# Attention operands stored per query tile, rows in alternating order, and a stepped priority for the second SwiGLU supertile's preparation

## The chip, the cores and the metric

The kernel runs on one core of a Trainium2 chip. The metric is the device time of one execution in microseconds (us). The engines are PE (TensorE: matmuls), PEld (its weight loads), DVE (VectorE), ACT (ScalarE), POOL (GpSimd) and SP (SyncE, which here issues every DMA). Each engine works through its own instruction list in order.

## The reference

One layer of a hybrid decoder trunk on x of 1 x 2048 x 1024, in float32:

```python
h = rmsnorm(x, norm1_g);  p = h @ w_in            # 1024 -> 2560 columns
u, (dq, dk, dv), (sq, sk, sv) = split(p)
a_out = pool_mixer(u)                             # 256 channels, windows 2, 4, 8, 16
# differential attention: 4 heads of two 64-wide softmax maps, 128-wide values, causal
b_out = rmsnorm((softmax(q1 k1^T) - lam * softmax(q2 k2^T)) v) * (1 - lam_init)
# stick-breaking attention: 4 heads of 64, strictly causal
c_out = rmsnorm((sigmoid(z) * prod of later (1 - sigmoid(z))) v)
x = x + concat(a_out, b_out, c_out) @ w_out
x = x + (silu(h2 @ w_gate) * (h2 @ w_up)) @ w_down   # h2 = rmsnorm(x, norm2_g), width 2816
return rmsnorm(x, final_norm_g)
```

## The kernel before

Every float32 product is made from split operands: a tile is written as a high part (rounded to fp32r) and a low part (the rest), ACT makes the first (L415), DVE the second (L416), and three matmuls (L474, L475, L476) make one product. The work is cut into query tiles of 512 rows, t = 0 to 3.

Stage one, `a1_tile`, makes the input projection for a tile: it transposes the normed x (L462) and goes through ten weight units in the order `UNITS[t]`. A unit holds 256 columns. Units 1, 2, 7 give q, units 3, 4, 8 give k, units 5, 6, 9 give v. Each half unit c ends in one PSUM bank, is split into a tile `st` of two halves (high, low), and is stored to DRAM (`q_d`, `k_d`: L611; `vd_d`, `vs_d`: L595).

Stage two, `attention`, goes through 24 pairs, six in each tile t, in the order `ORDER[t]`; this text counts them from 0, so that pairs 6 to 11 are those of t = 1. A pair is two maps of 64 channels (r = 0, 1): pairs p = 0 to 3 are differential heads, 4 and 5 are two stick-breaking heads each. `load_q` fetches q (L626), `load_kv` fetches k (L635) and v (L640, L645) for every key tile j up to t. `scores` makes a block of 128 queries (g = 0 to 3) against up to 512 keys with two matmuls: the first (L657) has the high part of q, the second (L658) the low part, and k holds its high part in partitions 0 to 63 and its low part in 64 to 127, while q's 64 rows stand twice. L700 ends a pair.

Stage three, `out_proj`, makes the output projection (L923 to L925). Stage four, `mlp`, is the SwiGLU in two supertiles of 1024 rows. A product of two by two blocks is made from seven smaller ones, so that operands are sums and differences of blocks (L961, mostly on POOL). While the gate and up products of the first supertile run, `head_out` prepares the operands of the second in 16 steps: 8 of `rows` (norm, transpose, store to `h_d`) and 8 of `operands` (load from `h_d` at L1064, subtract on POOL at L1070, split, store at L1080). `head_in` loads them later (L1098).

No order is written by hand. `Plan.op` records every operation with an estimated duration, a priority and its tiles; `Plan.schedule` plays the engines through with those estimates, takes on each engine the ready operation with the lowest priority number, and the instructions are issued in the order of the planned starts. Tiles come from rings of slots: a tile can be written when an earlier holder of its slot is no longer used. SP is in order too, so a DMA that waits holds up the DMAs behind it.

For q there are two rings of two slots, one for the high part and one for the low part. One slot of each (12 and 13) lies on the weight buffers of stage one and comes free only when stage one is done, in the course of pair 18:

```python
q0=ring([2, TQ], F32R, ("w", [31, 12])), q1=ring([2, TQ], F32R, ("w", [32, 13])),
wr=ring([4, 256], F32, ("w", R(12, 14)))      # of stage one
def dma_ns(nbytes): return max(nbytes / 360.0, 450.0)
```

Of the kernel before, what the change touches and what calls it, by code (L numbers as in the profile page):

```python
# [10 lines left out]
F32 = mybir.dt.float32  # L11
# [264 lines left out]
def hybrid_block_kernel(  # L276
# [23 lines left out]

    q_d = [dram.tile([2, P, S], F32, name=f"q_d{p}") for p in range(PAIRS)]
    k_d = [dram.tile([2, P, S], F32, name=f"k_d{p}") for p in range(PAIRS)]
    vd_d = [dram.tile([P, S // P, 2, P], F32, name=f"vd_d{p}") for p in range(DIFF_PAIRS)]
    vs_d = [dram.tile([P, S // P, 2, 64], F32, name=f"vs_d{p}") for p in range(2 * SB_PAIRS)]
    o_d = [dram.tile([KB, P, TQ], F32, name=f"o_d{t}") for t in range(NT)]
# [228 lines left out]
    def a1_tile(pl, rg, t, prio, prio_pe, first):  # L534
# [10 lines left out]
        if t == 0:  # L545
            constants(pl, {"w": rb["q1"], "h": rb["p0"]}, prio + 0.5, xs[3:])
        late = []
        for un in UNITS[t]:
# [30 lines left out]
            for c, ps in enumerate(pend):  # L579
                if un == 0:  # L580
                    late = pend
                    break
                st = rg["st"].new()
                if is_v:
                    nh, e = (2, 128) if un != 9 else (4, 64)
                    stv = lambda st=st, nh=nh: st.t.rearrange("p a (h b l e) -> p (a h) b l e", h=nh // 2, b=2, l=2)
                    pv = lambda ps=ps, nh=nh: ps.t.rearrange("p (b h e) -> p b h e", b=2, h=nh)
                    for h in range(nh):
                        split(pl, lambda h=h, stv=stv: stv()[:, h, :, 0, :], lambda h=h, stv=stv: stv()[:, h, :, 1, :],
                              lambda h=h, pv=pv: pv()[:, :, h, :], TQ // nh, True, [ps], (st, (h, 0)), (st, (h, 1)),  # L590
                              prio)
                        dst = vs_d[h] if un == 9 else vd_d[2 * (un - 5) + h]
                        pr = DIFF_PAIRS + h // 2 if un == 9 else 2 * (un - 5) + h
                        blk0 = 4 * t + 2 * c
                        pl.op("dma", dma_ns(P * 4096 // nh), lambda dst=dst, blk0=blk0, h=h, stv=stv: nc.sync.dma_start(  # L595
                            dst[:, blk0:blk0 + 2, :, :], f32(stv()[:, h])), r=[(st, (h, 0)), (st, (h, 1))],
                            w=[(m_v[pr][t], (c, h))], prio=prio)
                else:
                    isq = un in (1, 2, 7)
                    if isq:  # L600
                        pl.op("act", act_ns(TQ), lambda st=st, ps=ps: nc.scalar.mul(st.t[:, 0, :], ps.t, 0.125),
                              r=[ps], w=[(st, 0)], prio=prio)
                        pl.op("dve", dve_ns(TQ), lambda st=st, ps=ps: nc.vector.scalar_tensor_tensor(
                            st.t[:, 1, :], ps.t, 0.125, f32(st.t[:, 0, :]), ALU.mult, ALU.subtract),
                            r=[ps, (st, 0)], w=[(st, 1)], prio=prio)
                    else:
                        split(pl, lambda st=st: st.t[:, 0, :], lambda st=st: st.t[:, 1, :], lambda ps=ps: ps.t,
                              TQ, True, [ps], (st, 0), (st, 1), prio)
                    pair = {1: 0, 2: 2, 7: 4, 3: 0, 4: 2, 8: 4}[un] + c
                    dst, mk = (q_d, m_q) if isq else (k_d, m_k)  # L610
                    pl.op("dma", dma_ns(P * 4096), lambda st=st, dst=dst[pair]: nc.sync.dma_start(  # L611
                        dst[:, :, t0:t0 + TQ].rearrange("l p t -> p l t"), f32(st.t)),
                        r=[st], w=[mk[pair][t]], prio=prio)
        for c, ps in enumerate(late):
# [7 lines left out]
    def load_q(pl, rg, t, p, prio):  # L622
        q = [rg["q0"].new(), rg["q1"].new()]
        for hl in range(2):
            for dup in range(2):
                pl.op("dma", dma_ns(64 * 4096) * 1.3, lambda hl=hl, dup=dup: nc.sync.dma_start(  # L626
                    f32(q[hl].t[64 * dup:64 * dup + 64]),
                    q_d[p][hl, :, t * TQ:(t + 1) * TQ].rearrange("(r d) t -> d r t", r=2)),
                    r=[m_q[p][t]], w=[(q[hl], dup)], prio=prio)
        return q  # L630

    def load_kv(pl, rg, p, j, prio):
        k, v = rg["k"].new(), rg["v"].new()
        for hl in range(2):
            pl.op("dma", dma_ns(64 * 4096) * 1.3, lambda hl=hl: nc.sync.dma_start(  # L635
                f32(k.t[64 * hl:64 * hl + 64]),
                k_d[p][hl, :, j * TQ:(j + 1) * TQ].rearrange("(r d) t -> d r t", r=2)),
                r=[m_k[p][j]], w=[(k, hl)], prio=prio)
        if p < DIFF_PAIRS:
            pl.op("dma", dma_ns(P * 4096), lambda: nc.sync.dma_start(  # L640
                f32(v.t), vd_d[p][:, 4 * j:4 * j + 4].rearrange("p b l e -> p (b l e)")),
                r=[m_v[p][j]], w=[v], prio=prio)
        else:
            for r in range(2):
                pl.op("dma", dma_ns(P * 2048), lambda r=r: nc.sync.dma_start(  # L645
                    f32(v.t[:, r * TQ:(r + 1) * TQ]),
                    vs_d[2 * (p - DIFF_PAIRS) + r][:, 4 * j:4 * j + 4].rearrange("p b l e -> p (b l e)")),
                    r=[m_v[p][j]], w=[(v, r)], prio=prio)
        return k, v

    def scores(pl, rg, q, kt, r, g, j, t, strict, prio):
        n = TQ if j < t else (g + 1) * P
        s = rg["s"].new()
        qs = slice(g * P, (g + 1) * P)

        def qk():
            nc.tensor.matmul(s.t[:, :n], q[0].t[:, r, qs], kt.t[:, r, :n], start=True, stop=False)  # L657
            nc.tensor.matmul(s.t[:, :n], q[1].t[:, r, qs], kt.t[:, r, :n], start=False, stop=j < t)  # L658
# [3 lines left out]
        pl.op("pe", 2 * mm_ns(n) + (60 if j == t else 0), qk, r=[*q, kt], w=[s], prio=prio)  # L662
        return s, n
# [299 lines left out]
    def mlp(pl, rg, prio0):  # L963
# [72 lines left out]
        def head_out(prio):  # L1036

            def rows(b):
                xb = rg["x"].new()
# [19 lines left out]

            def operands(kk, c):  # L1060
                raw, tt = rg["x"].new([4, 256], F32), rg["x"].new([4, 256], F32)
# [21 lines left out]

            return [lambda b=b: rows(b) for b in range(8)] + [
                lambda kk=kk, c=c: operands(kk, c) for kk in range(4) for c in range(2)]

# [289 lines left out]
    def banks(ids):  # L1376
# [96 lines left out]
```

## Time and profile before

| | |
|---|---|
| runs | 2711.99, 2718.97 and 2724.35 us; median 2718.97 |
| the profiled execution's own time | 2719.03 us |
| its span in the trace | 2717.2 us, 39503 instructions |
| PE busy | 2601.9 us, 96% of the span |
| mean granted clock of PE | 0.977 of full speed |
| DVE, ACT, POOL busy | 66%, 49%, 32% |
| DMA | 454.27 MB, mean 167 GB/s |

The profile describes one execution. [...]

### The profile page before, as it was taken

The page shows a single profiled execution, that of the slowest core. Times are in us where ns is not written, and L with a number is a line of the kernel's source. Part 1 is how long each engine was busy: PE and PEld are TensorE (multiplying, and loading weights), DVE is VectorE, ACT ScalarE, POOL GpSimd, SP SyncE. Part 2 cuts the span into 40 slices and gives each one's busy share as a digit, 9 for nine tenths or more (in the row PEclk, how much of TensorE's full clock was granted, in tenths as well). Part 3 has the DMA queues.
Part 4 walks back from the last instruction along what each step waited for, and adds up shares of the span by engine and source line. Part 5 has one row for each costly group of instructions (what it writes and reads, how often), then busy time and mean ns, then how long its engine had stood idle before and what let it go on. Part 6 is the DMA issues. An engine that isn't in the chain of part 4 may idle for free.

```text
span 2717.2 us, 39503 instructions
## 1 busy us (share of the span) xinstructions
PE 2601.9 (96%) x13836; PEld 2176.7 (80%) x13836; DVE 1786.2 (66%) x3131; ACT 1319.3 (49%) x2645; POOL 870.0 (32%) x890
## 2 busy tenths in 40 slices
PE   9989989989999999999989999999999998999998
PEld 7878778877888788888978877888888886888886
DVE  6366787758887888788656666545444447558557
ACT  4365566646666666665534444323333333445444
POOL 1001212212254124133015456535454544132041
PEclk9989999989999999999999999999999999999999
DMA  6786585556564775664534457465222338335223
GB/s 217 245 251 184 160 245 160 155 155 202 153 177 147 225 203 147 192 178 161 166 118 155 155 184 239 158 220 199 101 102 97 109 129 291 118 95 194 93 90 120
DMA packets 223480, 454.27 MB, mean 167 GB/s; under 512 B 23720, under 2 KB 70952, under 8 KB 223280
## 3 DMA queue, kind: packets, MB, share of 16 engines
q1 hardware_dynamic: 223280, 451.75, 52.9%
q8 instruction: 108, 1.77, 0.3%
q14 instruction: 92, 0.75, 0.1%
HBM read 321.11 MB, written 130.55 MB: 166 GB/s over the span
## 4 chain that ended last, share of the span: by engine, by line
PE 72%; DMA 9%; DVE 9%; issue 3%; ACT 2%; POOL 1%; SPq 1%; DVEq 0%; ACTq 0%; POOLq 0%
PE bank L474 16%; PE bank L476 16%; PE bank L475 16%; DVE d L416 4%; DMA d<-q_d 4%; PE bank L657 3%; PE bank L681 3%; PE bank L658 3%; DMA d<-wo_d 2%; PE bank L924 2%; PE bank L923 2%; PE bank L925 2%; ACT d L415 1%; PE bank L562 1%; PE bank L781 1%
## 5 line engine op out<-in xcount | busy, mean ns | idle before, releaser
L474 PE MATMUL bank<-d 128*128 128x512 f32 x2296 | 919.0, 400 | 14.0 <-DVE d L1122 9.8
L476 PE MATMUL bank<-d 128*128 128x512 f32 x2296 | 910.3, 396 | 5.7 <-DVE d L416 5.4
L416 DVE TENSOR_TENSOR d<-d 128x512 fp32r<-128x512 f32 (+2 forms) x672 | 614.6, 938 | 457.5 <-ACT d L415 281.2
L475 PE MATMUL bank<-d 128*128 128x512 f32 x2296 | 909.3, 396 | 3.4 <-DVE d L416 3.4
L415 ACT CAST d<-d 128x512 fp32r<-128x512 f32 (+2 forms) x672 | 489.0, 758 | 651.0 <-PE bank L476 352.3
L961 POOL TENSOR_TENSOR d<-d 128x512 f32<-128x512 f32 x336 | 520.0, 1556 | 846.3 <-DVE d L416 622.9
L474 PEld LDWEIGHTS bank<-d 128*128 128x128 f32 x2296 | 435.7, 190 | 116.0 <-DVE d L1122 12.4
L476 PEld LDWEIGHTS bank<-d 128*128 128x128 f32 x2296 | 434.3, 189 | 110.3 <-DVE d L416 8.7
L475 PEld LDWEIGHTS bank<-d 128*128 128x128 f32 x2296 | 434.8, 189 | 101.3 <-DVE d L416 5.1
L416 DVE TENSOR_TENSOR d<-bank,d 128x512 fp32r<-128x512 f32 (+3 forms) x381 | 219.3, 603 | 139.7 <-ACT d L415 138.7
L819 POOL TENSOR_TENSOR d<-d 128x512 f32<-128x512 f32 (+3 forms) x160 | 160.4, 1003 | 397.9 <-DVE d L815 375.6
L415 ACT CAST d<-bank 128x512 fp32r<-128x512 f32 (+3 forms) x381 | 187.5, 529 | 194.0 <-PE bank L681 122.0
L729 ACT ACTIVATE d<-bank,d 128x512 f32<-128x512 f32 (+3 forms) x320 | 198.9, 627 | 128.4 <-DVE d L726 120.3
L751 POOL TENSOR_SCALAR d<-d 128x512 f32<-128x512 f32 (+3 forms) x144 | 95.8, 681 | 448.7 <-ACT d L741 318.1
L726 DVE TENSOR_REDUCE d<-bank 128x1 f32<-128x512 f32 (+3 forms) x320 | 186.9, 602 | 61.6 <-PE bank L658 31.1
L657 PE MATMUL bank<-d 128*128 128x512 f32 (+3 forms) x480 | 203.7, 425 | 24.8 <-ACT d L729 9.0
L658 PE MATMUL bank<-d 128*128 128x512 f32 (+3 forms) x480 | 181.9, 382 | 25.5 <-DMA d<-q_d 25.5
L1122 DVE TENSOR_TENSOR d<-bank,d 128x512 f32<-128x512 f32 x176 | 121.0, 687 | 116.0 <-PE bank L476 98.7
L815 DVE TENSOR_TENSOR_SCAN d<-d,bank 128x512 f32<-128x512 f32 (+3 forms) x160 | 174.3, 1090 | 19.6 <-ACT d L807 8.1
L1118 ACT COPY d<-bank 128x512 f32<-128x512 f32 x132 | 77.3, 586 | 221.7 <-PE bank L476 196.9
L681 PE MATMUL bank<-ident,d 128*128 128x128 f32 x1088 | 157.5, 279 | 3.4 <-DVE d L772 2.6
L923 PE MATMUL bank<-d 128*128 128x256 f32 x512 | 149.5, 292 | 2.8 <-DMA d<-wo_d 1.1
(133 smaller groups left out, 3593.5 us busy)
## 6 DMA issues: line engine op xcount, KB each, us to landing
d<-in_w_gu_dram SPq DMA_DIRECT2D x88, 512.0 KB, 3.5
d<-in_w_in_dram SPq DMA_DIRECT2D x80, 512.0 KB, 4.6
d<-k_d SPq DMA_DIRECT2D x120, 256.0 KB, 6.6
d<-wo_d SPq DMA_DIRECT2D x52, 512.0 KB, 6.0
d<-q_d SPq DMA_DIRECT2D x96, 256.0 KB, 6.3
d<-vd_d SPq DMA_DIRECT2D x40, 512.0 KB, 4.9
g_d<-d SPq DMA_DIRECT2D x66, 256.0 KB, 2.1
d<-g_d SPq DMA_DIRECT2D x66, 256.0 KB, 2.7
```

Source lines behind the costliest of these rows:

```text
L415: pl.op("act", act_ns(n, psum), lambda: nc.scalar.copy(hi(), src()), r=r, w=[whi], prio=prio)
L416: pl.op("dve", dve_ns(n), lambda: nc.vector.tensor_sub(lo(), src(), f32(hi())), r=[*r, *after, whi], w=[wlo], prio=prio)
L474: nc.tensor.matmul(o, a_hi, b_hi, start=first, stop=False, **kw)
L475: nc.tensor.matmul(o, a_hi, b_lo, start=False, stop=False, **kw)
L476: nc.tensor.matmul(o, a_lo, b_hi, start=False, stop=last, **kw)
L657: nc.tensor.matmul(s.t[:, :n], q[0].t[:, r, qs], kt.t[:, r, :n], start=True, stop=False)
L658: nc.tensor.matmul(s.t[:, :n], q[1].t[:, r, qs], kt.t[:, r, :n], start=False, stop=j < t)
L681: nc.tensor.transpose(tp.t[:, c:c + P], rows[qb][kb // 4].t[:, (kb % 4) * P:(kb % 4 + 1) * P], ident)
L726: pl.op("dve", dve_ns(n), lambda s=s, n=n, mc=mc, sm=sm: nc.vector.tensor_reduce(sm.t[:, mc:mc + 1], s.t[:, :n], AX, ALU.max, negate=True) ...
L729: pl.op("act", act_ns(n, True, 2), lambda s=s, n=n, e=e, mc=mc, lc=lc, sm=sm: nc.scalar.activation(e.t[:, :n], s.t[:, :n], AF.Exp, bias=sm ...
L923: nc.tensor.matmul(o, m[:, 0, cs], wh.t[:, k % 4, :], start=k == 0, stop=False)
L961: pl.op(eng, ns, lambda: en.tensor_tensor(out(), a(), b(), op), r=r, w=w, prio=prio)
```

## The change

The DRAM copies of q, k and v are made one tensor per pair and tile t, laid out as the load wants them: each partition's row is one run of 4096 bytes.

- q is no longer split into a tile of high and a tile of low parts but into two tiles by query half: h = 0 has the query blocks g = 0, 1, h = 1 has g = 2, 3, each with both parts. One ring of four slots takes the place of the two rings of two. A tile is loaded by one DMA of 128 partitions, in which each of the 64 rows is read twice, so that partitions 2d and 2d + 1 hold the same row.
- k stands in the order 2d (high), 2d + 1 (low), and is loaded by one DMA of 128 partitions where two of 64 partitions were needed. Values of the stick-breaking pairs take one load where they took two.
- The stores of q and k become two DMAs of 64 partitions (one for each r) where there was one of 128.
- In all: q loads 96 to 48, k loads 120 to 60, `vs_d` loads 40 to 20, stores of q and k 48 to 96. The bytes are the same. The estimates handed to the planner change with them, so the planner's order changes everywhere.
- `head_out`: step i of the 16 gets the priority of the first step plus i; before, all had the same.

```diff
-    q_d = [dram.tile([2, P, S], F32, name=f"q_d{p}") for p in range(PAIRS)]
-    k_d = [dram.tile([2, P, S], F32, name=f"k_d{p}") for p in range(PAIRS)]
+    q_d = [[dram.tile([2, 64, 2, 2, 256], F32, name=f"q_d{p}_{t}") for t in range(NT)] for p in range(PAIRS)]
+    k_d = [[dram.tile([64, 2, 2, TQ], F32, name=f"k_d{p}_{t}") for t in range(NT)] for p in range(PAIRS)]
...
-                    pl.op("dma", dma_ns(P * 4096), lambda st=st, dst=dst[pair]: nc.sync.dma_start(
-                        dst[:, :, t0:t0 + TQ].rearrange("l p t -> p l t"), f32(st.t)),
-                        r=[st], w=[mk[pair][t]], prio=prio)
+                    for r in range(2):
+                        pl.op("dma", dma_ns(P * 2048), lambda st=st, dst=dst[pair][t], r=r, isq=isq: nc.sync.dma_start(
+                            dst[:, :, r].rearrange("h d l t -> d h (l t)") if isq else dst[:, :, r],
+                            f32(st.t[64 * r:64 * r + 64])), r=[st], w=[(mk[pair][t], r)], prio=prio)
...
-        q = [rg["q0"].new(), rg["q1"].new()]
-        for hl in range(2):
-            for dup in range(2):
-                pl.op("dma", dma_ns(64 * 4096) * 1.3, lambda hl=hl, dup=dup: nc.sync.dma_start(
+        q = []
+        for h in range(2):
+            qh = rg["q"].new()
+            q.append(qh)
+            pl.op("dma", dma_ns(P * 4096), lambda h=h, qh=qh: nc.sync.dma_start(
+                f32(qh.t), q_d[p][t][h].rearrange("(d o) r l t -> d o (r l t)", o=1).to_broadcast([64, 2, D])),
+                r=[m_q[p][t]], w=[qh], prio=prio)
...
-        for hl in range(2):
-            pl.op("dma", dma_ns(64 * 4096) * 1.3, lambda hl=hl: nc.sync.dma_start(
+        pl.op("dma", dma_ns(P * 4096), lambda: nc.sync.dma_start(
+            f32(k.t), k_d[p][j].rearrange("d l r t -> (d l) r t")), r=[m_k[p][j]], w=[k], prio=prio)
...
-            return [lambda b=b: rows(b) for b in range(8)] + [
-                lambda kk=kk, c=c: operands(kk, c) for kk in range(4) for c in range(2)]
+            return [lambda b=b: rows(b, prio + b) for b in range(8)] + [
+                lambda kk=kk, c=c: operands(kk, c, prio + 8 + 2 * kk + c) for kk in range(4) for c in range(2)]
...
-        q0=ring([2, TQ], F32R, ("w", [31, 12])), q1=ring([2, TQ], F32R, ("w", [32, 13])),
+        q=ring([D], F32R, ("w", [31, 32, 12, 13])),
```

The line numbers of `scores` move from L657, L658 to L648, L649, of the q and k stores from L611 to L613, of the q loads from L626 to L630, of the k loads from L635 to L637.

How the order moves, at three places. First PE at the turn from pair 7 to pair 8 (t = 1). Before, d_3213 and d_3245 are pair 7's high and low parts of q, d_3584 and d_3609 those of pair 8, in the same slots:

```order
L657 MATMUL bank2_166<-d_3035,d_3213 128x512
L658 MATMUL bank2_166<-d_3035,d_3245 128x512
L660 LDWEIGHTS identb_116
L660 MATMUL bank2_166<-masks_118,identb_116 128x128
L474 MATMUL bank0_158<-d_1441,d_3080 128x512
...
L782 MATMUL bank7_186<-d_3625,d_2857 128x128
L657 MATMUL bank3_170<-d_3187,d_3584 128x512
L658 MATMUL bank3_170<-d_3187,d_3609 128x512
```

Now, d_3108 and d_3244 are pair 7's two query halves and d_3372 is pair 8's first, which takes the slot of d_3108:

```order
L649 MATMUL bank3_222<-d_3083,d_3108 128x256
L651 LDWEIGHTS identb_168
L651 MATMUL bank3_222<-masks_170,identb_168 128x128
...
L648 MATMUL bank4_226<-d_3063,d_3244 128x512
...
L649 MATMUL bank2_218<-d_3083,d_3244 128x512
L651 LDWEIGHTS identb_168
L651 MATMUL bank2_218<-masks_170,identb_168 128x128
L648 MATMUL bank3_222<-d_3211,d_3372 128x512
```

Between the last use of the old q and the first use of the new in the same slot lie 50 matmuls before and 74 now. Over pairs 6 to 18 the median of this number goes from 50 (29 to 128) to 122 (41 to 207, for both halves).

Second, SP where k of pair 0 at t = 1 is stored and fetched. Before, d_2959 is that k, in two loads:

```order
L611 DMA k_d0_66<-d_2925 128x2x512
L635 DMA d_2959<-k_d0_66 64x2x512
L412 DMA d_2970<-in_w_in_dram 128x1024
L611 DMA k_d1_67<-d_2957 128x2x512
L412 DMA d_2987<-in_w_in_dram 128x1024
L635 DMA d_2959<-k_d0_66 64x2x512
```

Now, d_3005 is that k:

```order
L613 DMA k_d0_1_85<-d_2970 128x1x512 x2
L637 DMA d_3005<-k_d0_1_85 128x1024
L412 DMA d_3018<-in_w_in_dram 128x1024
L613 DMA k_d1_1_89<-d_3003 128x1x512 x2
L412 DMA d_3043<-in_w_in_dram 128x1024
```

The second load of before stood behind the store of the next k; it is gone. On PE, the matmuls between the last product of a fresh q or k and its first use are fewer now: for k of pair 0 from 60 to 39 at t = 1 and from 76 to 40 at t = 2, for k of p = 2 at t = 2 from 60 to 40, for q of p = 0 at t = 1 from 144 to 59, and for q of p = 2 at t = 2 from 95 to 58.

Third, PE where the last k of t = 1 (p = 5) is made and used for the first time. Now, d_3994 and d_4012 are the weights of that unit, d_4420 is the k tile:

```order
L476 MATMUL bank0_210<-d_1581,d_4012 128x512
L462 MATMUL bank1_214<-ident_163,d_1629 128x128
...
L691 MATMUL bank5_230<-ones_c_179,d_4365 128x1 x4
...
L462 MATMUL bank1_214<-ident_163,d_1702 128x128
L648 MATMUL bank2_218<-d_4420,d_4281 128x128
L649 MATMUL bank2_218<-d_4420,d_4281 128x128
```

Only 28 transposes and the 4 sums of L691 stand between the two; before, about 200 matmuls stood there, from the input projection of the next tile and from pair 9. The attention has caught up with the stage that feeds it.

In the SwiGLU, the 8 `operands` steps stand spread over 12 loads of gate and up weights on SP before and over 15 now.

## Rows read from the trace of the kernel before

**Rows 1.** Busy time, projection and attention: length, engines' busy, granted clock, DMA share, GB/s.
```profile
0.00:1290.00 1290.00, 1213.73 (x7564) 1047.55 (x7564) 958.81 (x1848) 762.98 (x1728) 319.77 (x522) 0.96 0.63 187
```
**Rows 2.** Waits of PE, whole span: us in total, times, longest.
```profile
PE bank L658 <- DMA d<-q_d: 25.5, 14, 3.7
PE bank L657 <- ACT d L729: 9.0, 13, 2.8
PE bank L657 <- DMA d<-k_d: 6.5, 3, 3.4
PE bank L657 <- DMA d<-q_d: 2.0, 3, 1.3
```
**Rows 3.** Waits of PE from 330 to 900 us.
```profile
PE bank L658 <- DMA d<-q_d: 21.7, 11, 3.7
```
**Rows 4.** Busy time of nine stretches behind waits for q; first, longest, sum.
```profile
199.70:206.50 6.80, 6.80 (x32) 6.28 (x32) 4.10 (x7) 3.72 (x10) 2.21 (x6) 0.50 0.61 220
...
578.60:588.80 10.20, 8.35 (x24) 6.93 (x25) 1.54 (x3) 1.56 (x4) 0.00 (x0) 0.50 0.49 176
...
sum 40.80, PE 38.49 PEld 34.78 DVE 15.36 ACT 14.00 POOL 4.09; mean PE 4.28 PEld 3.86 DVE 1.71 ACT 1.56 POOL 0.45
```
**Rows 5.** Timeline of PE around the longest wait: start us, length us.
```profile
580.45 0.77 PE L658 MATMUL bank<-d 128*128 128x512 f32 x1 [3.70 <-DMA d<-q_d]
581.01 0.63 PE L657 MATMUL bank<-d 128*128 128x512 f32 x1
581.44 0.63 PE L658 MATMUL bank<-d 128*128 128x512 f32 x1
```
**Rows 6.** DMA issues, whole span: count, size of one, median us to landing.
```profile
d<-q_d SPq DMA_DIRECT2D x96, 256.0 KB, 6.3
d<-vd_d SPq DMA_DIRECT2D x40, 512.0 KB, 4.9
```
**Rows 7.** Issues of the q loads on SP: ns min/median/max.
```profile
L626 SPq DMA_DIRECT2D d<-q_d x96: 573/580/1285, 38.3 to 1149.7; - x96
```
**Rows 8.** Timeline of SP at k of pair 0, t = 1.
```profile
274.22 0.37 SPq L611 DMA_DIRECT2D k_d<-d  x1
276.99 0.58 SPq L635 DMA_DIRECT2D d<-k_d  x1
...
281.52 1.88 SPq L635 DMA_DIRECT2D d<-k_d  x3
```
**Rows 9.** Timeline of PE there.
```profile
285.83 0.39 PE L475 MATMUL bank<-d 128*128 128x512 f32 x1
286.05 0.39 PE L476 MATMUL bank<-d 128*128 128x512 f32 x1
289.09 0.44 PE L657 MATMUL bank<-d 128*128 128x128 f32 x1 [2.65 <-DMA d<-k_d]
```
**Rows 10.** Busy time of two stretches behind waits for k: their sum.
```profile
sum 10.20, PE 9.59 PEld 8.00 DVE 4.95 ACT 3.86 POOL 0.00; mean PE 4.79 PEld 4.00 DVE 2.47 ACT 1.93 POOL 0.00
```
**Rows 11.** Groups by line: count, busy us, mean ns of one, idle before.
```profile
L416 DVE TENSOR_TENSOR d<-bank,d 128x512 fp32r<-128x512 f32 (+3 forms) x381 | 219.3, 603 | 139.7 <-ACT d L415 138.7
L415 ACT CAST d<-bank 128x512 fp32r<-128x512 f32 (+3 forms) x381 | 187.5, 529 | 194.0 <-PE bank L681 122.0
L462 PE MATMUL bank<-ident,d 128*128 128x128 f32 x128 | 22.8, 313 | 7.7 <-DVE d L467 4.9 <-DVE d L450 2.3 <-DVE d L738 0.6
```
**Rows 12.** Busy time of two stretches with much DMA: loads to 64 partitions; to 128.
```profile
570.00:578.60 8.60, 6.75 (x46) 5.91 (x44) 2.99 (x5) 2.99 (x6) 0.00 (x0) 1.00 1.03 261
1802.00:1848.00 46.00, 46.00 (x200) 37.31 (x199) 21.93 (x22) 15.01 (x21) 21.02 (x16) 1.00 0.96 347
```
**Rows 13.** Waits from 1590 to 1710 us; and the clock behind two of them.
```profile
POOL d L1070 <- DMA d<-h_d: 13.8, 8, 6.9
PE bank L474 <- DVE d L1122: 8.5, 4, 3.7
sum 6.80, PE 6.80 PEld 5.28 DVE 5.95 ACT 2.00 POOL 2.90; mean PE 3.40 PEld 2.64 DVE 2.97 ACT 1.00 POOL 1.45
```

More of the change, by code (lines that the diff above doesn't have):

```diff
@@ L299, in hybrid_block_kernel @@
     dram = ctx.enter_context(tc.tile_pool(name="dram", bufs=1, space=bass.MemoryType.DRAM))
-    q_d = [dram.tile([2, P, S], F32, name=f"q_d{p}") for p in range(PAIRS)]
-    k_d = [dram.tile([2, P, S], F32, name=f"k_d{p}") for p in range(PAIRS)]
-    vd_d = [dram.tile([P, S // P, 2, P], F32, name=f"vd_d{p}") for p in range(DIFF_PAIRS)]
-    vs_d = [dram.tile([P, S // P, 2, 64], F32, name=f"vs_d{p}") for p in range(2 * SB_PAIRS)]
+    q_d = [[dram.tile([2, 64, 2, 2, 256], F32, name=f"q_d{p}_{t}") for t in range(NT)] for p in range(PAIRS)]
+    k_d = [[dram.tile([64, 2, 2, TQ], F32, name=f"k_d{p}_{t}") for t in range(NT)] for p in range(PAIRS)]
+    v_d = [[dram.tile([P, D], F32, name=f"v_d{p}_{t}") for t in range(NT)] for p in range(PAIRS)]
     o_d = [dram.tile([KB, P, TQ], F32, name=f"o_d{t}") for t in range(NT)]
@@ L545, in a1_tile @@
         if t == 0:
-            constants(pl, {"w": rb["q1"], "h": rb["p0"]}, prio + 0.5, xs[3:])
+            constants(pl, {"w": rb["q"], "h": rb["p0"]}, prio + 0.5, xs[3:])
         late = []
@@ L591, in a1_tile @@
                               prio)
-                        dst = vs_d[h] if un == 9 else vd_d[2 * (un - 5) + h]
                         pr = DIFF_PAIRS + h // 2 if un == 9 else 2 * (un - 5) + h
[L594 to L597, printed above, removed]
+                        o0, w = (h % 2 * TQ if un == 9 else 0) + 4 * c * e, 4 * e
+                        pl.op("dma", dma_ns(P * 4096 // nh), lambda dst=v_d[pr][t], o0=o0, w=w, h=h, stv=stv: nc.sync.dma_start(
+                            dst[:, o0:o0 + w], f32(stv()[:, h].rearrange("p b l e -> p (b l e)"))),
+                            r=[(st, (h, 0)), (st, (h, 1))], w=[(m_v[pr][t], (c, h))], prio=prio)
                 else:
@@ L600, in a1_tile @@
                     if isq:
-                        pl.op("act", act_ns(TQ), lambda st=st, ps=ps: nc.scalar.mul(st.t[:, 0, :], ps.t, 0.125),
+                        part = lambda l, st=st: st.t.rearrange("p h (l t) -> p h l t", l=2)[:, :, l, :]
+                        src = lambda ps=ps: ps.t.rearrange("p (h t) -> p h t", h=2)
+                        pl.op("act", act_ns(TQ), lambda part=part, src=src: nc.scalar.mul(part(0), src(), 0.125),
                               r=[ps], w=[(st, 0)], prio=prio)
-                        pl.op("dve", dve_ns(TQ), lambda st=st, ps=ps: nc.vector.scalar_tensor_tensor(
-                            st.t[:, 1, :], ps.t, 0.125, f32(st.t[:, 0, :]), ALU.mult, ALU.subtract),
+                        pl.op("dve", dve_ns(TQ), lambda part=part, src=src: nc.vector.scalar_tensor_tensor(
+                            part(1), src(), 0.125, f32(part(0)), ALU.mult, ALU.subtract),
                             r=[ps, (st, 0)], w=[(st, 1)], prio=prio)
@@ L622, in load_q @@
     def load_q(pl, rg, t, p, prio):
-        q = [rg["q0"].new(), rg["q1"].new()]
-        for hl in range(2):
-            for dup in range(2):
-                pl.op("dma", dma_ns(64 * 4096) * 1.3, lambda hl=hl, dup=dup: nc.sync.dma_start(
-                    f32(q[hl].t[64 * dup:64 * dup + 64]),
-                    q_d[p][hl, :, t * TQ:(t + 1) * TQ].rearrange("(r d) t -> d r t", r=2)),
-                    r=[m_q[p][t]], w=[(q[hl], dup)], prio=prio)
+        q = []
[5 more added lines that the diff above has]
+                r=[m_q[p][t]], w=[qh], prio=prio)
         return q
@@ L633, in load_kv @@
         k, v = rg["k"].new(), rg["v"].new()
-        for hl in range(2):
-            pl.op("dma", dma_ns(64 * 4096) * 1.3, lambda hl=hl: nc.sync.dma_start(
[L636 to L648, printed above, removed]
+        pl.op("dma", dma_ns(P * 4096), lambda: nc.sync.dma_start(
+            f32(k.t), k_d[p][j].rearrange("d l r t -> (d l) r t")), r=[m_k[p][j]], w=[k], prio=prio)
+        pl.op("dma", dma_ns(P * 4096), lambda: nc.sync.dma_start(f32(v.t), v_d[p][j]), r=[m_v[p][j]], w=[v], prio=prio)
         return k, v
@@ L653, in scores @@
         s = rg["s"].new()
-        qs = slice(g * P, (g + 1) * P)
+        qh, c0 = q[g // 2], 2 * r * 256 + g % 2 * P
         def qk():
-            nc.tensor.matmul(s.t[:, :n], q[0].t[:, r, qs], kt.t[:, r, :n], start=True, stop=False)
-            nc.tensor.matmul(s.t[:, :n], q[1].t[:, r, qs], kt.t[:, r, :n], start=False, stop=j < t)
+            nc.tensor.matmul(s.t[:, :n], qh.t[:, c0:c0 + P], kt.t[:, r, :n], start=True, stop=False)
+            nc.tensor.matmul(s.t[:, :n], qh.t[:, c0 + 256:c0 + 256 + P], kt.t[:, r, :n], start=False, stop=j < t)
             if j == t:
                 nc.tensor.matmul(s.t[:, n - P:n], identb, masks[:, strict, :], start=False, stop=True)
-        pl.op("pe", 2 * mm_ns(n) + (60 if j == t else 0), qk, r=[*q, kt], w=[s], prio=prio)
+        pl.op("pe", 2 * mm_ns(n) + (60 if j == t else 0), qk, r=[qh, kt], w=[s], prio=prio)
         return s, n
@@ L1036, in head_out, with rows @@
         def head_out(prio):
-            def rows(b):
+            def rows(b, prio):
                 xb = rg["x"].new()
@@ L1058, in rows, with operands @@
                     h_d[:, :, b * P:(b + 1) * P].rearrange("k p t -> p k t"), ht.t), r=[ht], w=[(m_h, b)], prio=prio)
-            def operands(kk, c):
+            def operands(kk, c, prio):
                 raw, tt = rg["x"].new([4, 256], F32), rg["x"].new([4, 256], F32)
```

## The prediction, made before the changed kernel was run

> **What bounds the kernel now.** I read the table of the profile first: PE is busy 96% of the span, so a change can win only where PE stands idle or runs at the lower clock. Then the busy time by stretch: projection and attention fill the first 1290 us, PE is busy there for 1213.7 us, and its mean granted clock is 0.96 [rows 1]. So some 76 us are idle, and 4% of the clock is another 52 us (0.04 of 1290), 128 us in all. The other engines have room (DVE 959 us of the 1290). Then the waits of PE: the greatest is L658 for the load of q, 25.5 us in 14 waits, and L657 adds 2.0 us for q and 6.5 us for k [rows 2]. L658 reads the low part, which is fetched last of the four q loads.
>
> A wait costs more than its own time. Behind the longest one (3.70 us) the next 512-column matmuls start 0.43 us apart [rows 5], against 0.22 us in full flow [rows 9]. [...] Nine such stretches stand behind waits for q, 40.8 us together [rows 4]; half of that, 20.4 us, is work lost. Waits for q thus cost 25.5 + 2.0 + 20.4 = 47.9 us. Waits for k cost 6.5 + 10.2 / 2 = 11.6 us [rows 2, 10].
>
> **Why q comes late.** Until stage one gives up slots 12 and 13 there is one slot for each part, so the loads for a pair start when the old pair has done its last scores. The four loads need three further issues of 0.58 us each [rows 7] before the last starts, and then 6.3 us to land [rows 6]: 8.0 us. In the order, a median of 50 matmuls of other work stands between release and use. At 1213.7 us / 7564, or 0.16 us each [rows 1], that is 8.0 us. Half of the pairs then come up short, and they do.
>
> **The change, part by part.** The times are summed against the profiled execution's own 2719.0 us, which is equal to the median of the runs shown.
>
> *q loads.* A half tile is released half a pair earlier, and a tile is needed only when its own half begins. From pair 6 on the median distance is now 122 matmuls, 19.5 us at 0.16 us. The need is one DMA of 512 KB; the nearest row is `vd_d`, the same size into 128 partitions with 4096-byte rows: 4.9 us [rows 6], 31 matmuls. Every distance from pair 6 on is over that (41 at the least). So the waits from 330 us on go: 21.7 us on L658 [rows 3], 2.0 us on L657 [rows 2], and half of 40.8 - 6.8 us of low clock [rows 4], 17.0 us. Term: -40.7 us. Three distances (41, 46, 46) are near the edge when the queue is full; I put back 1 us of wait and 1.7 us of clock for each: +8. The early waits (25.5 - 21.7 = 3.8 us, and 3.4 us of clock) lie in t = 0, where distances stay at 37 to 97 matmuls. I leave them as they are; bounds -7 to +7.
>
> *k and q that are used fresh.* Here the new order is tighter. A chain runs from the last product through ACT (0.53) and DVE (0.60) [rows 11], the store (274.22 to 276.99, when the load that waits for it goes out: 2.8 us) [rows 8] and the load (4.9 us) [rows 6]: 9.2 us. The store is now two DMAs of 64 partitions. What that costs is not shown for a store, so I take it from loads: into 64 partitions the queue moved 261 GB/s at full share, into 128 it moved 347 [rows 12]. For 512 KB that is 2.0 against 1.5 us, and a second issue of 0.37 us [rows 8] comes to it: +0.9, so 10.1 us; bounds 9.2 and 16.0 (below). Against it stand 39, 40, 40, 59 and 58 matmuls of mixed size, which by the columns in the order (0.22 to 0.23 us for 512 [rows 9]) make 9.0, 8.4, 8.4, 7.7 and 9.2 us of work. The missing time is 1.1 + 1.7 + 1.7 + 2.4 + 0.9 = 7.8 us. For the last k of t = 1 there are 28 transposes at 22.8 / 128 = 0.18 us [rows 11] and the sums, some 6 us: 4.1 us are missing. Together 11.9 us of idle time, and behind the four over 1.3 us a low stretch of the mean length in rows 4 (40.8 / 9 = 4.5 us, half lost): 9. That is 21 where the waits for k cost 11.6: +9. It is no more because the second k load, which went out 4.5 us behind the first [rows 8] and made PE wait 2.65 us [rows 9], is gone.
>
> *SP and DMA.* Issues fall by 48 + 60 + 20 - 48 = 80. SP is not what PE waits for, apart from the chains above: nothing taken. A q store that moves from one DMA to two has 0.37 us behind it on SP, hidden by the 59 and more matmuls to its use; without that cover it is in the chain above.
>
> *The splits of q into the new layout.* Same elements on ACT and DVE (48 instructions); at nothing, since DVE has over 300 us of room [rows 1]. If two short runs cost 0.1 us each it would be 5 us on DVE, still off PE's path.
>
> *The SwiGLU.* From 1590 to 1710 us PE waits 8.5 us for DVE L1122, since POOL stands before L1070 until `h_d` lands (13.8 us) and what is behind it on POOL, the sums of the next weights, comes late to DVE; the clock adds 6.8 / 2 = 3.4 us [rows 13]. The priorities only stretch the eight steps from 12 weight loads to 15. The loads of `h_d` still go out just ahead of their use. I take 0.4 of 11.9 us: -5; bounds -12 (all) and +3 (one more wait of the longest kind, 3.7 us).
>
> Sum: -40.7 + 8 + 9 - 5 = -29, so 2719 - 29 = 2690 us.
>
> [...]
>
> **Rivals.** *B, slower: the fresh chains decide.* If a chain takes as long as the one in rows 8 and 9 did, from 274.22 to 289.09, 14.9 us, with the 1.1 us of ACT and DVE 16.0 us, the missing times are 7.0, 7.6, 7.6, 8.3, 6.8 and 10.0, 47 us, and the clock behind each like the longest stretch (10.2 / 2) another 31: 78 - 11.6 = +66. Then 2719 - 40.7 + 8 + 66 - 5 = 2747. Each us of chain is worth 6 us of idle time; with the clock the change turns to a loss at some 13.5 us. For it: at 281.52 the loads took 7.5 us in a full queue. Against it: the interposed load is gone.
>
> *C, given back.* The pairs turn over faster, and PE then waits for ACT and DVE instead, as it already does at L657 for L729 (9.0 us, 13 waits) [rows 2]. If half of the 40.7 goes that way and the SwiGLU gains nothing: 2719 - 20.4 + 8 + 9 = 2715. For it: 959 us of DVE work would stand in fewer us. Against it: there are still 300 to spare.
>
> *D, more.* The wide loads shorten the queue for all: no waits for q at any pair, none for k, all of the SwiGLU's: -47.9 - 11.6 - 11.9 = -71, 2648; half way to it 2669.
>
> **How the numbers follow.** Forecast (2675 to 2705) 0.55, B 0.10, C 0.22, D 0.13. Half a per cent, 13.6 us, is about what a measurement tells from no change. Faster: the forecast, D: 0.68. Same: C, 0.22. Slower: B, 0.10. The range takes in D's half way and C's end: 2660 to 2718, and leaves out B and the far end of D. The forecast's own is 2675 to 2705.
>
> **What would show it.** In the new profile: L649 and L648 waiting for q under 10 us in all; the mean clock of the first stretch 0.97 or more; waits for k of 8 to 16 us, one of them 3 to 5 us long near 500 us at the first use of the last k of t = 1; POOL still waiting for `h_d`. I am wrong if the waits for k exceed 30 us (B), or if those for q go and PE's idle time before 1290 us stays over 65 us (C).

## The result, and the profile after

The changed kernel takes 2697.4 us (median of four runs, 2692.7 to 2700.4) against 2720.2 us for the kernel before on the same chip (four runs). The ratio is 0.9918, 95% interval 0.989 to 0.9947. The profiled execution took 2698.9 us, with a span of 2697.1 us and a mean granted clock of 0.98. The forecast was 2690 us.

Most of it is won in projection and attention. The first stretch of the changed kernel, in the columns of [rows 1]:

```profile
0.00:1290.00 1290.00, 1222.40 (x7789) 1055.33 (x7790) 975.90 (x1904) 783.62 (x1757) 328.46 (x522) 0.97 0.58 191
```

PE issues 225 matmuls more in the same 1290 us. It is idle for 67.6 us there (1290 less 1222.40), against 76.3 us, and the clock is 0.97 against 0.96. The waits of PE over the whole span of the changed kernel, to lay beside [rows 2] (L658 and L657 are now L649 and L648):

```profile
PE bank L474 <- DVE d L1113: 13.6, 6, 4.6
PE bank L648 <- ACT d L720: 11.1, 12, 4.2
PE bank L648 <- DMA d<-k_d: 7.1, 4, 4.3
PE bank L648 <- DVE d L806: 6.5, 8, 2.3
PE bank L915 <- DMA d<-wo_d: 6.1, 6, 2.3
PE bank L882 <- DVE d L887: 6.1, 2, 5.7
PE bank L462 <- DVE d L467: 5.5, 4, 1.7
PE bank L672 <- DVE d L763: 5.0, 6, 1.6
```

No line of the view, further down either, names `q_d`: the 27.5 us of waits for q are gone to the last one. What grew is under the names of ACT and DVE. The same view of the kernel before, cut to 0 to 1290 us, has these for L648 <- DVE L806, L672 <- DVE L763 and L882 <- DVE L887:

```profile
PE bank L657 <- DVE d L815: 2.9, 8, 0.7
PE bank L681 <- DVE d L772: 2.6, 5, 0.8
PE bank L891 <- DVE d L896: 0.5, 1, 0.5
```

These three and the wait for ACT (9.0 us in [rows 2]) went from 15.0 to 28.7 us: half of the 27.5 came back there. In all, more came back: idle time before 1290 us fell by only 8.7 us.

All stretches before 1290 us at a granted clock of 0.50, summed: first the kernel before (20 stretches), then the changed one (9).

```profile
sum 102.50, PE 95.06 PEld 80.70 DVE 58.34 ACT 40.89 POOL 12.24; mean PE 4.75 PEld 4.04 DVE 2.92 ACT 2.04 POOL 0.61
```
```profile
sum 71.90, PE 56.77 PEld 45.07 DVE 47.25 ACT 30.17 POOL 8.65; mean PE 6.31 PEld 5.01 DVE 5.25 ACT 3.35 POOL 0.96
```

What the lower clock costs is estimated as half of PE's busy time in these stretches, since in the changed kernel 512-column matmuls start 0.43 us apart from 702.1 us on, at a granted clock of 0.50, and 0.23 us apart from 387.2 us on, at 1.00: 47.5 us before and 28.4 us now, 19.1 us less. (The length of the stretches, 102.5 and 71.9 us, holds idle time too, and that is counted already.) With the 8.7 us of idle time this makes 27.8 us by 1290 us.

The loads answer to [rows 6] (DMA issues: count, size, median us to landing):

```profile
d<-v_d SPq DMA_DIRECT2D x60, 512.0 KB, 4.2
d<-k_d SPq DMA_DIRECT2D x60, 512.0 KB, 4.8
d<-q_d SPq DMA_DIRECT2D x48, 512.0 KB, 4.7
```

After attention part of the gain is given up. The last product of the output projection starts at 1376.40 us in the kernel before, 1347.54 us in the changed one, 28.9 us earlier (timelines of PE):

```profile
1376.40 0.28 PE L925 MATMUL bank<-d 128*128 128x256 f32 x1
```
```profile
1347.54 0.28 PE L916 MATMUL bank<-d 128*128 128x256 f32 x1
```

The span ends only 20.1 us earlier: from that product to its end are 1340.8 us before and 1349.6 us now. From 1559 to 1730 us, where the SwiGLU's second supertile is prepared, the waits that [rows 13] show for the kernel before are now these:

```profile
POOL d L1061 <- DMA d<-h_d: 34.7, 8, 7.7
```
```profile
PE bank L474 <- DVE d L1113: 12.7, 5, 4.6
```

POOL's waits for `h_d` are 2.5 times as long, and PE's wait for DVE behind them has risen from 8.5 to 12.7 us. In 180 us from 1590 us (before) and from 1560 us (now) PE's idle time is 9.2 and 16.2 us, its granted clock 0.98 and 0.95.

### The profile page after: what moved, and what is told of

Same layout as the page of the kernel before. It is cut to its first block, busy times and chain, and to the rows that moved or that the text cites. A ratio compares the mean times of both kernels' runs of the same rounds, so it can differ in the third digit from the quotient of the medians.

```text
span 2697.1 us, 39409 instructions
## 1 busy us (share of the span) xinstructions
PE 2585.4 (96%) x13836; PEld 2162.4 (80%) x13836; DVE 1780.7 (66%) x3131; ACT 1325.5 (49%) x2649; POOL 877.6 (33%) x890
## 4 chain that ended last, share of the span: by engine, by line
PE 57%; DVE 9%; DMA 6%; ACT 4%; issue 3%; POOL 2%; SPq 1%; DVEq 0%; POOLq 0%; ACTq 0%
PE bank L474 14%; PE bank L476 14%; PE bank L475 14%; DVE d L416 4%; PE bank L672 3%; PE bank L648 2%; POOL d L952 2%; DVE d L806 2%; ACT d L415 2%; PE bank L649 2%; PE bank L915 1%; PE bank L914 1%; PE bank L916 1%; DMA d<-wo_d 1%; PE bank L817 1%
## 5 line engine op out<-in xcount | busy, mean ns | idle before, releaser
L416 DVE TENSOR_TENSOR d<-d 128x512 fp32r<-128x512 f32 (+1 forms) x672 | 622.1, 948 | 463.2 <-ACT d L415 281.5
L415 ACT CAST d<-d 128x512 fp32r<-128x512 f32 (+1 forms) x672 | 490.0, 758 | 665.0 <-PE bank L476 356.6
L416 DVE TENSOR_TENSOR d<-bank,d 128x512 fp32r<-128x512 f32 (+4 forms) x381 | 220.1, 604 | 113.9 <-ACT d L415 109.2
L415 ACT CAST d<-bank 128x512 fp32r<-128x512 f32 (+4 forms) x381 | 187.7, 527 | 188.3 <-PE bank L672 107.7
L742 POOL TENSOR_SCALAR d<-d 128x512 f32<-128x512 f32 (+3 forms) x144 | 103.3, 734 | 440.1 <-ACT d L732 394.1
L648 PE MATMUL bank<-d 128*128 128x512 f32 (+3 forms) x480 | 200.0, 417 | 28.9 <-ACT d L720 11.1
L806 DVE TENSOR_TENSOR_SCAN d<-d,bank 128x512 f32<-128x512 f32 (+3 forms) x160 | 174.5, 1091 | 32.0 <-ACT d L798 13.7
L1113 DVE TENSOR_TENSOR d<-bank,d 128x512 f32<-128x512 f32 x176 | 121.1, 688 | 112.7 <-PE bank L476 93.7
L649 PE MATMUL bank<-d 128*128 128x512 f32 (+3 forms) x480 | 176.5, 370 | 0.0
L672 PE MATMUL bank<-ident,d 128*128 128x128 f32 x1088 | 155.9, 276 | 6.0 <-DVE d L763 5.0
```

What stands on the lines that cost most here:

```text
L415: pl.op("act", act_ns(n, psum), lambda: nc.scalar.copy(hi(), src()), r=r, w=[whi], prio=prio)
L416: pl.op("dve", dve_ns(n), lambda: nc.vector.tensor_sub(lo(), src(), f32(hi())), r=[*r, *after, whi], w=[wlo], prio=prio)
L648: nc.tensor.matmul(s.t[:, :n], qh.t[:, c0:c0 + P], kt.t[:, r, :n], start=True, stop=False)
L649: nc.tensor.matmul(s.t[:, :n], qh.t[:, c0 + 256:c0 + 256 + P], kt.t[:, r, :n], start=False, stop=j < t)
L672: nc.tensor.transpose(tp.t[:, c:c + P], rows[qb][kb // 4].t[:, (kb % 4) * P:(kb % 4 + 1) * P], ident)
L806: pl.op("dve", scan_ns(n), lambda iv=iv, n=n, w=w, s=s, prev=prev: nc.vector.tensor_tensor_scan(iv.t[:, n - 1::-1], w.t[:, n - 1::-1], s.t ...
```

## The experiments

Two questions stood open. Does each part of the change do what the sum said (first two runs)? And what removes the waits for q and makes the time: the earlier release of half a tile, as the prediction argues, or the load itself, now one DMA of 128 partitions instead of two of 64? The runs came in three groups, each on another chip, and each group has its own runs of the kernel before (2718.7, 2720.5 and 2726.6 us). Across groups medians and ratios can therefore say different things, and both are given. In the third group (loads cut by columns, order alone, k planned late) they differ by 11 to 13 us.

### Each part alone

The attention part alone has one priority for the preparation again:

```
-            return [lambda b=b: rows(b, prio + b) for b in range(8)] + [
-                lambda kk=kk, c=c: operands(kk, c, prio + 8 + 2 * kk + c) for ...
+            return [lambda b=b: rows(b, prio) for b in range(8)] + [
+                lambda kk=kk, c=c: operands(kk, c, prio) for ...
```

> The changed kernel with all 16 preparation steps at one priority again, so the attention part alone. Theory T (the attention part gained 31 us by the start of the SwiGLU, and the stepped priority gave 11 back): 2686 us, between 2680 and 2692; PE waits for the sums of gate and up (L1113) under 10 us. Rival R (the priority does nothing by itself, and the SwiGLU lost its 11 us because the planner's order changed with everything else): 2697 us, between 2693 and 2701.

The priority part alone is the kernel before with the first two lines in place of the last two.

> The kernel before with the stepped priority alone. T: 11 us slower than before, 2731 us (2726 to 2736), more waits of PE for L1122 between 1550 and 1770 us. R: within 4 us of 2719.

Attention alone: 2689.7 us, ratio 0.9902 [0.9878, 0.9925]. Priority alone: 2726.2 us, ratio 1.0039 [1.0023, 1.0054]. By the medians the stepped priority costs 7.7 us on top of the new attention and 7.4 us on top of the old (4 and 11 by the ratios; of the two only the second stands clear of the noise by itself). The traces agree with the medians. The last product of the output projection, first attention alone (span 2685.7 us), then priority alone (span 2727.0 us):

```profile
1345.60 0.28 PE L916 MATMUL bank<-d 128*128 128x256 f32 x1
```
```profile
1377.35 0.28 PE L925 MATMUL bank<-d 128*128 128x256 f32 x1
```

From there to the end are 1340.1 us with one priority and 1349.6 us with steps, where the kernel before has 1340.8 us and the changed one 1349.6 us: some 9 us each time, and so the two parts add up. Theory T, which had 11 us, holds in both runs, in the second at the edge of its bounds (2726 to 2736); rival R falls. POOL's wait for `h_d` in the same stage follows the priority, not the attention; first attention alone, then priority alone:

```profile
POOL d L1061 <- DMA d<-h_d: 15.8, 8, 7.9
```
```profile
POOL d L1070 <- DMA d<-h_d: 34.4, 8, 7.8
```

### Release or width

Attention alone, with each load of q and k as two DMAs of 64 partitions; the planner is told of both:

```
+            for dup in range(2):
+                pl.op("dma", dma_ns(64 * 4096), lambda ...: nc.sync.dma_start(
+                    f32(qh.t[64 * dup:64 * dup + 64]), q_d[p][t][h].rearrange("d r l t -> d (r l t)")),
...
+        for hl in range(2):
+            pl.op("dma", dma_ns(64 * 4096), lambda hl=hl: nc.sync.dma_start(
+                f32(k.t[64 * hl:64 * hl + 64]), k_d[p][j][:, hl]), ...
```

> The attention part alone, but every q half tile and every k tile is loaded by two DMAs of 64 partitions, as before the change; q tiles by query half stay. If the earlier release is what removed the waits for q: waits for q under 8 us and a time within 8 us of the attention part alone. If the width of the loads did it: waits for q of 15 us and more, and 16 us or more above the attention part alone.

Attention alone, with q cut into its high and low tile as before (two rings, released together), each loaded by one DMA of 128 partitions:

```
-            qh = rg["q"].new()
+        q = [rg["q0"].new(), rg["q1"].new()]
...
+                f32(q[hl].t.rearrange("p r t -> p (r t)")),
+                q_d[p][t][hl].rearrange("(d o) r t -> d o (r t)", o=1).to_broadcast([64, 2, D])),
```

> The attention part alone, with wide single loads of q and k, but q in a tile of high and a tile of low parts in two rings, as before. If the earlier release is needed: waits for q of 10 us and more, and 10 us or more above the attention part alone. If the wide load suffices (0.3 us of issue and 4.9 us against some 8 us of other work): waits for q under 5 us and a time within 6 us of the attention part alone.

Narrow loads with halves: 2731.7 us, ratio 1.004 [1.0018, 1.0062], slower than before the change. Wide loads without halves: 2695.9 us, ratio 0.9923 [0.9903, 0.9944], 22.9 of the 29.0 us of attention alone. The 6 us between the two are not clear of the noise, and the order is another one here too. The waits of PE, first with narrow loads, then without halves (L646 is its second matmul, L645 its first):

```profile
PE bank L650 <- DMA d<-k_d: 21.3, 8, 5.2
...
PE bank L650 <- DMA d<-q_d: 3.9, 2, 3.1
```
```profile
PE bank L646 <- DMA d<-q_d: 6.5, 9, 1.0
PE bank L645 <- DMA d<-k_d: 3.6, 3, 1.9
```

So with narrow loads the earlier release does take q's waits away, 27.5 to 3.9 us, but in this order no time is won: k's waits rise to 21.3. Each theory named for the narrow run has half of it, the release the waits and the width the time. Without the release the waits for q are many and short, none over 1.0 us; the 6.5 us lie between the two forecasts for that run.

The narrow run had one flaw: its plan with two loads gave PE another order. The next two keep the order of attention alone row for row on PE and DVE (their traces have it on ACT and POOL too), and only issue two DMAs in the planned step. In the second of them q stays wide; its k tile holds its rows in another order than its q tiles, so its scores are not the reference's, while instructions and sizes are.

```
-        pl.op("dma", dma_ns(P * 4096), lambda: nc.sync.dma_start(
-            f32(k.t), k_d[p][j].rearrange("d l r t -> (d l) r t")), ...
+        pl.op("dma", dma_ns(P * 4096), lambda: [nc.sync.dma_start(
+            f32(k.t[64 * hl:64 * hl + 64]), k_d[p][j][:, hl]) for hl in range(2)], ...
```

> The attention part alone, with every load of a q half tile and of a k tile issued as two of 64 partitions in the same planned step, so that the order of TensorE's and VectorE's instructions is that of the attention part alone, row for row; only SyncE's issues double. The earlier narrow run had also been given another order by the planner, so that its 42 us may be the order's. Theory T2: width is what makes the time: k waits over 15 us, about 2725 us. Rival O: the 42 us were mostly the order's, with the same order the narrow loads cost some 10 us: 2700 us.

> As the run before, but only the k loads are narrow, q's stay whole; the order of TensorE and VectorE is again that of the attention part alone. If the k tiles' width is what counts (theory K: their chain from store to first use is the tight one), the time is within 5 us of the run with both narrow. If q's width counts (theory Q), it is within 5 us of the attention part alone, 2690 us. If both are traffic on the same queue and add up, it lies half way.

Both narrow: 2708.2 us, ratio 0.9961 [0.9938, 0.9983]. Only k narrow: 2705.5 us, 0.9946 [0.9926, 0.9965]. With the order held, narrow loads cost 18.5 us by the medians (16 by the ratios), neither the 42 of the first narrow run nor 10, so that both T2 (2725 us) and rival O (2700 us) miss. k's alone cost 16 of them (12 by the ratios): theory K. Theory Q falls. In waits, first both narrow, then k alone:

```profile
PE bank L648 <- DMA d<-k_d: 10.3, 7, 3.9
...
PE bank L648 <- DMA d<-q_d: 2.9, 2, 1.6
```
```profile
PE bank L648 <- DMA d<-k_d: 14.4, 9, 3.7
```

Is it the partitions, or only that there are twice as many DMAs? The next run has two DMAs of 128 partitions and half the columns:

```
+        pl.op("dma", dma_ns(P * 4096), lambda: [nc.sync.dma_start(f32(k.t[:, r, :]),
+            k_d[p][j][:, :, r].rearrange("d l t -> (d l) t")) for r in range(2)], ...
```

> The attention part alone, with every load of a q half tile and of a k tile issued as two of 128 partitions and half the columns in the same planned step. As many issues, and as many bytes in each, as in the run with both loads narrow (2708 us), in the same order of TensorE and VectorE; only the number of partitions differs. If the number of partitions is what costs (theory T3), the time is that of the attention part alone, 2690 us, at most 2695. If it is the number of issues (rival I: SyncE's time and its place in the queue), it is 2708 us.

2692.9 us, ratio 0.9873 [0.9838, 0.9907]: 3 us over attention alone by the medians, 8 us under it by the ratios, and by either clearly under the run with both narrow. So it is the partitions (T3), not the number of issues. Nor is it the length of the rows in DRAM: they are 2048 bytes here, and 4096 bytes in the narrow run. The last product of the output projection, both narrow and then both cut by columns (1345.60 us in attention alone):

```profile
1368.34 0.28 PE L916 MATMUL bank<-d 128*128 128x256 f32 x1
```
```profile
1354.14 0.28 PE L916 MATMUL bank<-d 128*128 128x256 f32 x1
```

The second of these executions (2698.6 us) was the slowest of its four.

The DMA issues, both narrow and then both cut by columns, have equal counts and sizes:

```profile
d<-k_d SPq DMA_DIRECT2D x120, 256.0 KB, 5.2
...
d<-q_d SPq DMA_DIRECT2D x96, 256.0 KB, 4.5
```
```profile
d<-k_d SPq DMA_DIRECT2D x120, 256.0 KB, 4.3
...
d<-q_d SPq DMA_DIRECT2D x96, 256.0 KB, 4.0
```

The line of k's load alone (L637), in the same order, tells the spread:

```profile
DMA to landing us min/median/max: 3.4/5.2/10.5
```
```profile
DMA to landing us min/median/max: 2.5/4.3/6.8
```

In the median 64 partitions cost 0.9 us a load of k and 0.5 us a load of q, but the slowest load of k lands after 10.5 instead of 6.8 us; with only k narrow it was 10.7 us. What makes the landings later with 64 partitions is not shown.

Last, what another order alone is worth: attention alone with the planner's cost of a v load raised by a tenth, which changes the order in many rows.

> The attention part alone, with the planner's cost of a v load raised by a tenth and nothing else: the same instructions, in an order that differs in many rows. It measures what another order alone can be worth. If the 23 us that lie between the two narrow runs are what any new order may cost (theory N), this run is over 5 us away from 2690 us. If an order made with the right costs is as good as another (theory M), it lies within 5 us, and the 23 us belong to the plan for two narrow loads in particular.

2690.1 us, ratio 0.9857 [0.9824, 0.9889]. By the medians this is theory M, 0.4 us from attention alone; by the ratios it is 12 us faster, which would be theory N, though the two intervals overlap. Either way this other order costs nothing. It is a weak test, though: counted in the traces by line, tile and shape, 554 of PE's 13836 matmuls stand in another place than in attention alone, and 2851 in the first narrow run. What the 23.5 us between the two narrow runs are thus stays open, beyond the waits for k that the traces show (21.3 against 10.3 us).

### The SwiGLU's waits

The changed kernel, and attention alone, with the loads of `h_d` planned to land 3 us later (`late` is added to the time at which the planner lets a load's users start):

```
+                c.ready = max(c.ready, o.end + self.lag(e, c.eng) + o.late)
...
                         raw.t[:, i, :], h_d[k, :, c0:c0 + 256]),
-                        r=[(m_h, c0 // P), (m_h, c0 // P + 1)], w=[(raw, i)], prio=prio)
+                        r=[(m_h, c0 // P), (m_h, c0 // P + 1)], w=[(raw, i)], prio=prio, late=3000.0)
```

> The changed kernel, with one number of the planner's: the loads of the transposed rows back from DRAM that the SwiGLU's operand step starts with are taken to land 3000 ns later than planned so far, so the subtractions that wait for them are put later in the engines' orders. Nothing is computed otherwise. Theory W: the stepped priority costs its 7.5 us (the two single-part runs agree on that) because GpSimd, and behind it VectorE and TensorE, stand in order in front of these subtractions until the rows have landed (GpSimd's waits for h_d were 34.7 us in 1559 to 1730 us, 13.8 before); planned later, GpSimd's wait falls below 15 us, TensorE's wait of the transposes for VectorE below 8 us, and the time is 2690 us. Rival V: the waits come of the order in which the rows and operands are asked for, or of VectorE's own load, and where the subtractions stand makes no difference: 2697 us.

> The attention part alone (uniform priority), with the same later landing time for the operand step's loads as the run beside it. Theory W: with the uniform priority GpSimd waited less for these loads, so there is less to win: 2686 us against 2690 of the attention part alone. Rival V: 2690 us, no change.

The changed kernel so planned takes 2678.7 us, ratio 0.9857 [0.9829, 0.9885]; attention alone 2675.8 us, 0.9844 [0.9818, 0.9869]. That is 18.8 and 13.9 us less by the medians (17 and 16 by the ratios), more than theory W asked for. In the first of them the subtractions on POOL no longer wait for those loads; POOL's waits from 1559 to 1730 us, and PE's (L1115 is L1113 before):

```profile
POOL d L954 <- DVE d L418: 61.2, 16, 10.7
POOL d L954 <- ACT d L417: 5.9, 1, 5.9
POOL d L954 <- DMA h_d<-d: 5.5, 1, 5.5
```
```profile
PE bank L476 <- DVE d L1115: 7.3, 5, 1.8
```

PE's wait for DVE falls from 12.7 to 7.3 us, the longest from 4.6 to 1.8. POOL itself stands idle no less than before (its waits in this window add up to 73.2 us, against 61.3 in the changed kernel), now mostly for DVE, so its idle time by itself is not what PE pays for. The last product of the output projection, the changed kernel so planned (span 2686.5 us) and attention alone so planned (span 2680.4 us):

```profile
1352.65 0.28 PE L918 MATMUL bank<-d 128*128 128x256 f32 x1
```
```profile
1349.26 0.28 PE L918 MATMUL bank<-d 128*128 128x256 f32 x1
```

From there to the end are 1333.9 us (1349.6 without the change to the plan) and 1331.1 us (1340.1 without). So 16 and 9 us are won behind the output projection, where these loads stand, and PE's order of matmuls is the same row for row in each pair of kernels. With the loads planned late, stepped and uniform priority lie 2.9 us apart by the medians instead of 7.7, and 2.7 us instead of 9.5 in this stretch of the traces. So the greater part of what the steps cost hangs on work that stands in order before loads that have not landed. That it goes through POOL alone is not shown: the new plan also moves some 70 instructions each of DVE and ACT.

### The waits for k

The fastest of these, with k's loads planned 3 us later too:

```
-            ..., r=[m_k[p][j]], w=[k], prio=prio)
+            ..., r=[m_k[p][j]], w=[k], prio=prio, late=3000.0)
```

> The fastest kernel so far (the attention part with the later landing time for the SwiGLU's operand loads, 2676 us), with the k tile's loads too taken to land 3000 ns later in the plan. It has 8.0 us of waits for k in 4 places. If these stand because the planner puts the first matmuls on a fresh k tile too early (theory W for k), they fall below 3 us and the time is about 2668 us. If the order around them has nothing else to put there (rival), the waits move to other names and the time stays at 2676 us.

2674.0 us, ratio 0.9794 [0.9753, 0.9835]: 1.8 us less by the medians, 14 by the ratios, and the two intervals overlap, so the size of a gain is not shown. Its 8.0 us of waits for k are gone, but two others have grown by 3.3 and 3.9 us, from 11.3 and 6.5 (the rows are those of this run). Over the whole span PE's idle time fell from some 104 to some 100 us in the two traces: half of the waits moved, as the rival has it, and half went. Between theory W and the rival this run does not decide.

```profile
PE bank L650 <- ACT d L722: 14.6, 13, 4.1
PE bank L884 <- DVE d L889: 10.4, 5, 8.7
```

## Why the prediction was right, and where it was not

**The total** came out right: 2697 in 2660 to 2718, on the side named. Luck has a part in it. Attention was to give -40.7 + 8 + 9 = -24 us; the first 1290 us gave 27.8, and attention alone gave 29.0 in the medians. Of the 24 us forecast, 15 were to be idle time (23.7 less 3 put back and 5.4 more for k) and 8 clock (17.0 less 5.1 put back and 4 behind k). Measured were 8.7 of idle time, and for the clock the low stretches give an estimated 19.1. What the sum put back for q and k hardly came, and what it left out, the waits for ACT and DVE, took its place. The 4 us too much in attention then hid a third of the miss in the SwiGLU.

**The q term had the right size for a reason that did not decide.** The step "A half tile is released half a pair earlier, and a tile is needed only when its own half begins" is the one that carried too much. The release is real and removes q's waits, but with narrow loads it leaves the kernel slower than before (2731.7 us) or 12 us faster (2708.2 us), by the order; wide loads without the release give 22.9 of 29 us. The sum used the wide load only as a need of 4.9 us (measured: 4.7) and gave it no credit for k, where most of it lies: with k's loads alone narrow, the waits for k are 14.4 us instead of the 5.8 of attention alone. The sum also counted half of the low stretches' whole length, with idle time inside them counted twice; half of PE's busy time in them [rows 4] gives 15.8 us instead of 17.0.

**Rival C was half true.** Its test, idle time over 65 us with q's waits gone, was met: 67.6 us. By the prediction's own sign the forecast was wrong there. Some 14 of 27.5 us came back as waits for ACT and DVE. It was not met in the time, because the low stretches fell from 102.5 to 71.9 us. The +8 put back for three short distances and the 3.8 us left at t = 0 were not needed: no wait for q stands anywhere. That much of rival D came true; its other two parts, no waits for k and none in the SwiGLU, did not.

**Fresh k** was right in kind: 7.1 us in 4 waits, just under the 8 to 16 named, and the long one stands at the first use of the last k of t = 1, at 401.5 us, not near 500. Timelines of SP and of PE there:

```profile
390.17 1.17 SPq L613 DMA_DIRECT2D k_d<-d  x2
392.23 0.34 SPq L412 DMA_DIRECT2D d<-in_w_in_dram  x1
395.23 1.28 SPq L637 DMA_DIRECT2D d<-k_d  x3
```
```profile
388.40 0.39 PE L476 MATMUL bank<-d 128*128 128x512 f32 x1
...
392.92 1.31 PE L462 MATMUL bank<-ident,d 128*128 128x128 f32 x8 [1.40 <-DVE d L467]
395.14 1.97 PE L462 MATMUL bank<-ident,d 128*128 128x128 f32 x8 [0.91 <-DVE d L467]
401.46 0.44 PE L648 MATMUL bank<-d 128*128 128x128 f32 x1 [4.34 <-DMA d<-k_d]
```

From the first store to the load are 5.1 us where I had 2.8 + 0.9, and from the load's issue to its use 6.2 where I had 4.9. That the wait was forecast at 4.1 us and measured 4.34 is chance: the chain is 2.7 us longer than the sum had, and the work beside it took some 8.3 us instead of 6, since the transposes themselves waited 2.5 us, most of it for DVE. In the other places less was missing than the sum had: 2.8 us in three waits against 7.8. Rival B, the chains at 16 us, is excluded. The 0.9 us for two narrow stores rests on a wrong reading of [rows 12]: in the stretch that stands there for loads to 64 partitions, SP issues two loads of q and three of v, and these are twice the size and go to 128 partitions (the kernel before):

```profile
571.09 1.24 SPq L626 DMA_DIRECT2D d<-q_d  x2
572.38 4.44 SPq L640 DMA_DIRECT2D d<-vd_d  x3
```

What the number of partitions costs a load is shown only by the two runs above, 0.9 and 0.5 us in the median; for a store no run shows it.

**The SwiGLU term had the wrong sign**: -5 forecast, +7.4 and +7.7 measured by the medians, some 9 in the traces. The failed step is "The priorities only stretch the eight steps from 12 weight loads to 15 ... I take 0.4 of 11.9 us". The bound of +3 allowed one more wait; what came were eight waits of POOL that grew from 13.8 to 34.7 us together. I had seen the cause (POOL before L1070 until `h_d` lands) and said that the loads still go out just ahead of their use; the sum should have drawn from it that a spread order doesn't help while the plan takes these loads to land too early. Why the steps make these waits longer, and not only no shorter, was not taken apart.

**SP and the splits** at nothing: twice the issues of q and k, cut by columns, cost at most 3 us by the medians, and the splits keep their median (DVE, the kernel before and then the changed one).

```profile
L603 DVE SCALAR_TENSOR_TENSOR d<-bank,d x24: 656/683/693, 29.1 to 868.7; 128x512 fp32r<-128x512 f32 x24
```
```profile
L604 DVE SCALAR_TENSOR_TENSOR d<-bank,d x24: 665/683/692, 29.5 to 850.5; 128x512 fp32r<-128x512 f32 x24
```

## What to carry to other kernels

When a load is split by partitions, try first to lay it out in DRAM so that each DMA fills all 128: here it was worth 16 to 18 us at the same order of work. For the earlier release of buffers 6 us were measured, not clear of the noise. Where a program is ordered ahead of time, look in the trace for engines that stand before a load (POOL for `h_d` here) and correct the planner's landing time for it; that one number was worth 14 to 19 us by the medians, 9 to 16 in the stretch it bears on, and a change of priorities around it lost 7 to 9. A wait that is removed must be followed to the names that take it over: at least half came back at once. And when waits are added up with a low clock, count only the busy time of the low stretches.

## What was not expected of the hardware

Two sets of loads with the same bytes, count and issuing steps differ little in the median (5.2 against 4.3 us to landing) but much at the slow end (10.5 against 6.8 us) when each reaches 64 instead of 128 partitions. The run with the faster landings has the shorter rows in DRAM, 2048 against 4096 bytes.
